# Grouped-query attention: another share of the exponentials for VectorE, and V in other units

## The chip, the cores and the metric

The kernel runs on one core of one Trainium2 chip. The time is the device time of one execution in microseconds; the median of several runs counts. The core's engines work side by side, each through its own queue in order: TensorE (PE) for matrix products, ScalarE (ACT), VectorE (DVE), GpSimd (POOL), and SyncE (SP), which here only starts transfers.

## The reference

Attention with shared keys and values: batch 8, 512 positions, 32 query heads, 8 key/value heads (four query heads share one), dimension 64, all in fp32.

```python
scores = np.einsum('bhqd,bhkd->bhqk', Q, K_expanded) * scale      # scale = 1/8
weights = np.exp(scores - np.max(scores, axis=-1, keepdims=True))
weights = weights / (np.sum(weights, axis=-1, keepdims=True) + 1e-10)
output = np.einsum('bhqk,bhkd->bhqd', weights, V_expanded)
```

## The kernel before, in words

The fast path (`fast_path`) leaves the maximum out, computes exp(scores) as it is, and checks at the end that all sums lay between 64 and 57344; if not, `general_path` computes everything again. The order of the work is written out by hand: each engine takes its instructions in the order of the program text.

**Jobs.** The work is 64 jobs, j = 0 to 63, eight for each batch entry, one for each key/value head. A job has two pairs of query heads, i = 0 and 1. For each pair, each of four key chunks kc and each head m of the pair there is one block of scores, 128 keys x 512 queries: 16 blocks in all. They come from TensorE into PSUM, and their exponentials go into the tile `pt` as fp16, keys on the partitions. Then TensorE multiplies `pt` with V (`pv`, L365): V has a 65th column of ones, so that each output carries the sum of its weights. Of a pair's 64 such matmuls, those that use the last-made blocks of `pt` come last (`blocks`, L358).

**Who makes the exponentials.** ScalarE makes most of them, two blocks at a time (`act_tile`, L296; L302), from the PSUM tiles `s_ps` (two buffers). The first two or three blocks of pair 1 are made otherwise (`WIDE`, L41: three in a wide job, which is 4 <= j < 62 with j % 5 != 2, 47 jobs; two in the others, here called narrow jobs). The steps of this second way are:

- `exp_d` (L306, L313): VectorE turns scores in the PSUM tile `d_ps` (one buffer) into the bits u of a rough fp16 exponential.
- `exp_d2` (L320): VectorE takes the fraction f (L325); GpSimd makes a factor g (L330) and the product w of g and f (L336). Where `odd` is true (L324: a wide job in front of a narrow one, and job 62), VectorE makes g, and only w is left to GpSimd.
- `exp_d4` (L346, L349): VectorE adds w to u, which gives the block of `pt`.

**The order in one job.** `exp_d4` of a job is done in the middle of the next job, and so are all its PV matmuls. In job j (L570 to L630, last = j - 1): ScalarE tile 0; two blocks for VectorE and their conversion; tile 1; a check; PV of pair 0 of the last job with tile 2's scores between its halves; `norm` (L402: the reciprocal of the sums at L417, and the product that empties the one PV buffer into `o_sb` at L422); tile 3; in a wide job the single half tile 4, in one bank of `d_ps`; the transposes of a later job's Q into the other bank (`trans_q`, L207); `exp_d4` of the last job; `exp_d2` of this job; the copy of the transposed Q (L220); g, where it is VectorE's; PV of pair 1 in pieces between tiles 5 and 6; where the next job is wide, the scores and the conversion of its third block (L622); `norm` of pair 1.

**Loads and checks.** Q, K and V come by DMAs that GpSimd issues and that convert to bf16, in jobs listed by hand (`LOADS`, L275). V goes straight into its padded tile `vt` (65 columns a head). K is transposed by DMAs of SP's queue (`dma_k`, L190, in the jobs of `KEYS`, L269). `check_v` (L236, L238) takes the largest magnitude of one chunk of V, 32 times. `check_sums` (L395, L388) compares 16 pairs' sums with the limits, every five jobs.

Of the kernel before, what the change touches and what calls it, by code (L numbers as in the profile page):

```python
# [33 lines left out]
SUM_LO = 64.0  # L34
SUM_HI = 57344.0
V_HI = 1.0e15
NLAST = 16
LAST_SUMS = NLAST * 2 * 4


WIDE = lambda j: 4 <= j < 62 and j % 5 != 2  # L41

# [25 lines left out]
def fast_path(ctx, tc, Q, K, V, out, flag, ident):  # L68
# [13 lines left out]
    const_pool = ctx.enter_context(tc.tile_pool(name="const", bufs=1))  # L82
    qnat_pool = ctx.enter_context(tc.tile_pool(name="qnat", bufs=4))
    knat_pool = ctx.enter_context(tc.tile_pool(name="knat", bufs=2))
    qt_pool = ctx.enter_context(tc.tile_pool(name="qt", bufs=3))
# [10 lines left out]

    ok = const_pool.tile([128, SPB * 2 * SC], FP32, name="ok")
    okv = const_pool.tile([128, B * SC], FP32, name="okv")
    okall = const_pool.tile([128, 1], FP32, name="okall")
# [4 lines left out]
    vt = [const_pool.tile([128, SC, KV, D + 1], BF16, name=f"v{j}") for j in range(2)]  # L104
# [4 lines left out]
    kn, qn, kt, qt, twice = {}, {}, {}, {}, {}  # L109

# [8 lines left out]

    def load_v(b, lo=0):  # L120
        to = vt[b % 2][:, :, lo:, 0:D]
        of = V[b, :, lo:, :].rearrange("(p sc) g d -> p sc g d", p=128)
        if lo:
            for sc in range(SC):
                nc.gpsimd.dma_start(out=to[:, sc], in_=of[:, sc])
        else:
            nc.gpsimd.dma_start(  # L127
                out=to.rearrange("p sc g d -> p (sc g) d"),
                in_=of.rearrange("p sc g d -> p (sc g) d"),
            )  # L130

# [103 lines left out]

    def check_v(b, sc):  # L236
        n = b * SC + sc
        nc.vector.tensor_reduce(  # L238
            out=okv[:, n:n + 1], in_=vt[b % 2][:, sc, :, 0:D], op=ALU.max, axis=AX.XY,
            apply_absolute_value=True,  # L240
        )

    NJOB = NU * 2
    DPAIR = NPAIR - 1

    def taken(j):
        return 3 if WIDE(j) else 2

# [3 lines left out]
    def act_tiles(j):  # L252
# [7 lines left out]

    CHECKS = {
        (j, at): divmod(n, SC) for n, (j, at) in enumerate(
            [(j, 0) for j in (3, 4, 6, 7, 8, 11, 12, 16, 17, 21, 22, 23, 26, 27, 31, 32)]
            + [(j, 0) for j in (36, 37, 38, 41, 42, 46, 47, 48, 51, 52, 56, 57, 60, 61, 62)]
            + [(62, 1)]
        )
    }

    KEYS = dict(zip((4, 10, 16, 26, 36, 41, 50), range(1, B)))  # L269

# [24 lines left out]

    def act_tile(j, n, spare=None):  # L296
        group = act_tiles(j)[n]
        i, kc, lo = group[0]
        ps = s_pool.tile([128, 2, S], FP32, name="s_ps") if spare is None else spare
        for _, _, m in group:  # L300
            scores(j, ps[:, m, :], i, kc, m)
        return nc.scalar.activation(  # L302
            out=jobs[j]["pt"][:, i, kc, lo:, :], in_=ps[:, lo:, :], func=EXP, scale=scale
        )

    def exp_d(j, lo, hi, ps, other=None):  # L306
        st = jobs.setdefault(j, {})
        if "u" not in st:
            for name, dtype in (("u", I16), ("f", I16), ("g", BF16), ("w", BF16)):
                st[name] = dve_pool.tile([128, 3, S], dtype, name=name + "16")[:, 0:taken(j), :]  # L310
        for n in range(lo, hi):
            apart(scores(j, ps[:, n - lo, :], DPAIR, *divmod(d_block(j) + n, 2)), other)
        return lambda: nc.vector.tensor_scalar(  # L313
            out=st["u"][:, lo:hi, :], in0=ps[:, 0:hi - lo, :], scalar1=A_U, scalar2=B_U,
            op0=ALU.mult, op1=ALU.add,
        )

    def exp_d2(j, engine=None):  # L320
        st = jobs[j]
        by_bits = engine is None
        engine = engine or nc.gpsimd
        odd = j == NJOB - 2 or WIDE(j) and not WIDE(j + 1)  # L324
        nc.vector.tensor_single_scalar(  # L325
            out=st["f"], in_=st["u"], scalar=1023, op=ALU.bitwise_and
        )

        def factor():
            (nc.vector if odd else engine).tensor_scalar(  # L330
                out=st["g"], in0=st["f"], scalar1=-EXP_F1,
                scalar2=EXP_K * 2.0 ** (24 * by_bits), op0=ALU.add, op1=ALU.mult,
            )

        def product():
            engine.tensor_tensor(  # L336
                out=st["w"], in0=st["g"], in1=st["f"].bitcast(FP16) if by_bits else st["f"],
                op=ALU.mult,
            )
# [25 lines left out]
    def pv(j, i, lo, hi):  # L365
# [9 lines left out]
        for n in range(lo, hi):  # L375
# [3 lines left out]
                st["pt"][:, i, kc, m, qc * 128:(qc + 1) * 128],  # L379
                vt[b % 2][:, kc, 2 * gp + g, :],  # L380
# [4 lines left out]
    def in_bounds(outs, inv, first):  # L385
        ops = ((1.0 / SUM_HI, ALU.is_ge), (1.0 / SUM_LO, ALU.is_le))
        for out_, in1, (bound, op) in zip(outs, (first, outs[0]), ops):
            nc.vector.scalar_tensor_tensor(  # L388
                out=out_, in0=inv, scalar=bound, in1=in1, op0=op, op1=ALU.mult
            )  # L390


    full = []

    def check_sums():  # L395
        while full:
            flat = invs.pop(full.pop()).rearrange("p s m qc -> p (s m qc)")
            in_bounds((ok, ok), flat, ok)

    inv_last = const_pool.tile([128, NLAST, 2, SC], FP32, name="inv_last")  # L400

    def norm(j, i):  # L402
# [31 lines left out]
        if left > NLAST and n == SPB - 1:  # L434
            full.append(k)

    def all_checks():
        assert not full and not invs
        vmax = const_pool.tile([128, 1], FP32, name="vmax")
        nc.vector.tensor_reduce(out=vmax, in_=okv, op=ALU.max, axis=AX.X)  # L440
        okmin = const_pool.tile([128, 1], FP32, name="okmin")
        nc.vector.tensor_reduce(out=okmin, in_=ok, op=ALU.min, axis=AX.X)
        nc.gpsimd.tensor_scalar(
            out=okall, in0=vmax, scalar1=V_HI, scalar2=okmin, op0=ALU.is_le, op1=ALU.mult
        )

    LIMITS = ((1.0 / SUM_HI, ALU.is_ge), (1.0 / SUM_LO, ALU.is_le))
    rights = [const_pool.tile([128, LAST_SUMS], BF16, name=f"right{n}") for n in range(2)]

    def last_rights(lo, hi, first=None):  # L450
        inv = inv_last.rearrange("p s m qc -> p (s m qc)")
        for engine, right, (bound, op) in zip((first or nc.gpsimd, nc.gpsimd), rights, LIMITS):
            engine.tensor_scalar(
                out=right[:, lo:hi], in0=inv[:, lo:hi],
                scalar1=bound, scalar2=okall, op0=op, op1=ALU.mult,
            )
# [39 lines left out]
    for j in range(2):  # L496
        nc.gpsimd.memset(vt[j][:, :, :, D:D + 1], 1.0)
    load_k(0, 2, 4)
    load_k(0, 4, KV)
    load_q(0, 8, 16)  # L500
    load_v_head(0, 1)
    load_v(0, 2)
    nc.gpsimd.memset(ones, 1.0)
    nc.gpsimd.memset(ok, 1.0)

# [51 lines left out]
    two_keys(1)  # L557
    exp_d(0, 0, 2, d_tile())()
    act_tile(0, 3)
# [10 lines left out]
    for j in range(1, NJOB - 1):  # L570
# [8 lines left out]
        if j == 1:  # L579
            dma_k(0, 2)  # L580
        if j in KEYS:
# [12 lines left out]
        pv(last, 0, 0, 16)  # L594
# [6 lines left out]
        bank = d_tile()  # L601
        beside = act_tile(j, 4, bank) if taken(j) > 2 else None

# [30 lines left out]
    act_tile(j, 0)  # L634
    exp_d(j, 0, 2, d_tile())()
    all_checks()
# [139 lines left out]
```

## Time and profile before

| what | value |
|---|---|
| median of 3 runs | 404.75 us (404.59 to 404.81) |
| the profiled execution | 404.57 us |
| its span, first to last instruction | 402.8 us |
| granted TensorE clock, mean | 0.999 |
| ACTIVATE of 128x1024 (L302) | x400, mean 1122 ns |
| ACTIVATE of 128x512 (L302) | x47, mean 724 ns |
| conversion of 128x512 (L313) | x47, mean 684 ns |
| g on GpSimd, 128x1536 (L330) | x35, mean 1470 ns |
| w on GpSimd, 128x1536 (L336) | x47, mean 3098 ns |
| g on VectorE, 128x1536 (L330) | x12, mean 551 ns |

A row of a timeline gives the start in microseconds from the span's start, the duration, the engine, the line, the operation, what it writes and reads, and how many instructions the row holds; in brackets, how long the engine stood idle before it and for whom. A row of groups gives the count, the busy time in all, the mean duration in ns, and the idle time before. A row of stretches gives the stretch and its length, then the busy time (and count) of PE, its weight loads, DVE, ACT and POOL, the granted clock, the share of the DMA engines and GB/s.

### The profile page before, as it was taken

How to read it: one execution, taken by the hardware profiler on the slowest of the kernel's cores; microseconds unless marked ns; L12 is line 12 of the kernel's file. 1: busy time of each engine (PE TensorE's matmuls, PEld its weight loads, DVE VectorE, ACT ScalarE, POOL GpSimd, SP SyncE). 2: the span in 40 equal slices, each digit the busy share in tenths (PEclk: the TensorE clock that was granted, in tenths of full speed). 3: DMA queues.
4: the chain of work that ended last, by engine and by line, in shares of the span. 5: the costliest groups of instructions: out<-in, count | busy, mean ns of one | idle time of the engine just before them, and what ended most of it. 6: DMA issues, size and time to landing. Idle time of an engine off the chain costs nothing.

```text
span 402.8 us, 12997 instructions
## 1 busy us (share of the span) xinstructions
PE 375.8 (93%) x5670; PEld 228.0 (57%) x5670; DVE 366.4 (91%) x635; ACT 393.9 (98%) x454; POOL 286.8 (71%) x169
## 2 busy tenths in 40 slices
PE   7999999999999999999999999999999999999985
PEld 3565555555555555555555555555555555556554
DVE  4788998999999999999999999999999999999996
ACT  5999999999999999999999999999999999999995
POOL 9848577597587687687687686677776767765752
PEclk9999999999999999999999999999999999999999
DMA  9979999899999259999259999679369959222206
GB/s 145 163 190 182 91 288 225 164 211 237 184 214 206 107 88 247 192 239 182 107 84 226 168 227 197 208 109 252 110 170 202 175 169 128 107 106 106 88 34 201
DMA packets 82893, 67.73 MB, mean 168 GB/s; under 512 B 52752, under 2 KB 57872, under 8 KB 82832
## 3 DMA queue, kind: packets, MB, share of 16 engines
q0 software_dynamic: 45072, 24.91, 48.3%
q1 hardware_dynamic: 36688, 41.49, 36.6%
q8 instruction: 45, 0.74, 0.7%
q10 hardware_dynamic: 1072, 0.46, 0.4%
q14 instruction: 16, 0.13, 0.1%
HBM read 50.33 MB, written 33.55 MB: 208 GB/s over the span
## 4 chain that ended last, share of the span: by engine, by line
ACT 29%; PE 25%; POOL 24%; DVE 20%; issue 2%; ACTq 0%; DVEq 0%
ACT pt L302 28%; POOL w L336 16%; PE pv L377 12%; PE s_ps L284 9%; POOL g L330 8%; DVE pt L349 8%; DVE o_sb L422 4%; DVE f L325 4%; DVE qt L220 2%; PE d_ps L215 2%; DVE g L330 1%; DVE inv L417 1%; PE d_ps L284 1%; PE s_ps L510 1%; PE d_ps L377 0%
## 5 line engine op out<-in xcount | busy, mean ns | idle before, releaser
L302 ACT ACTIVATE pt<-s_ps 128x1024 f16<-128x1024 f32 x400 | 379.0, 1122 | 0.3 <-PE s_ps L284 0.2
L336 POOL TENSOR_TENSOR w<-g,f 128x1536 bf16<-128x1536 bf16 (+1 forms) x63 | 179.6, 2851 | 37.6 <-DVE g L330 33.4
L377 PEld LDWEIGHTS <-pt 128*128 128x128 f16 x4096 | 142.1, 98 | 81.2 <-issue 41.6
L377 PE MATMUL pv<-v,pt 128*128 128x65 bf16 x4032 | 177.8, 195 | 3.7 <-DVE o_sb L422 2.2
L284 PE MATMUL s_ps<-qt,kt 64*128 64x512 bf16 x746 | 152.3, 384 | 12.0 <-ACT pt L302 10.0
L330 POOL TENSOR_SCALAR g<-f 128x1536 bf16<-128x1536 int16 (+1 forms) x50 | 67.1, 1341 | 69.1 <-DVE f L325 69.0
L313 DVE TENSOR_SCALAR u<-d_ps 128x1024 int16<-128x1024 f32 (+1 forms) x111 | 109.9, 990 | 0.3
L284 PEld LDWEIGHTS <-kt 64*128 64x128 bf16 x960 | 50.2, 93 | 55.3 <-issue 31.5
L422 DVE TENSOR_TENSOR o_sb<-pv,inv 128x512 f32<-128x512 f32 x112 | 77.5, 692 | 3.9
L284 PE MATMUL d_ps<-qt,kt 64*128 64x512 bf16 x214 | 58.4, 376 | 3.5 <-ACT pt L302 0.3
L349 DVE TENSOR_TENSOR pt<-u,w 128x1536 uint16<-128x1536 int16 (+1 forms) x64 | 56.4, 882 | 2.3 <-POOL w L336 0.2
L220 DVE COPY qt<-d_ps 128x1024 bf16<-128x1024 bf16 x62 | 42.3, 684 | 0.0
L215 PEld LDWEIGHTS <-q_nat 128*128 128x128 bf16 x508 | 28.5, 98 | 23.8 <-issue 23.8
L417 DVE RECIPROCAL inv<-pv 128x8 f32<-128x8 f32 x112 | 23.1, 207 | 17.4 <-PE pv L377 16.0
L215 PE MATMUL d_ps<-ident,q_nat 128*128 128x128 bf16 x496 | 38.3, 220 | 0.0
L302 ACT ACTIVATE pt<-d_ps 128x512 f16<-128x512 f32 x47 | 34.0, 724 | 0.0
L325 DVE TENSOR_SCALAR f<-u 128x1536 int16<-128x1536 int16 (+1 forms) x64 | 33.3, 521 | 0.0
L238 DVE TENSOR_REDUCE okv<-v 128x1 f32<-128x512 bf16 x32 | 21.6, 676 | 0.0
L142 POOL DMA_DIRECT2D q_nat<-in_Q_dram x19 | 15.2, 801 | 0.1
L284 PE MATMUL s_ps<-qt,kt_first 64*128 64x512 bf16 x56 | 11.1, 396 | 1.9 <-ACT pt L302 1.5
L127 POOL DMA_DIRECT2D v<-in_V_dram x7 | 12.3, 1753 | 0.0
L422 DVE TENSOR_TENSOR o_sb<-pv,inv_last 128x512 f32<-128x512 f32 x14 | 9.7, 692 | 0.5
(61 smaller groups left out, 62.7 us busy)
## 6 DMA issues: line engine op xcount, KB each, us to landing
out_dram<-o_sb SPq DMA_DIRECT2D x31, 1024.0 KB, 6.1
q_nat<-in_Q_dram POOLq DMA_DIRECT2D x14, 1024.0 KB, 12.4
k_nat<-in_K_dram POOLq DMA_DIRECT2D x7, 512.0 KB, 7.5
v<-in_V_dram POOLq DMA_DIRECT2D x7, 512.0 KB, 13.6
kt<-kt SPq DMA_DIRECT2D x14, 256.0 KB, 4.0
q_nat<-in_Q_dram POOLq DMA_DIRECT2D x3, 512.0 KB, 7.5
out_dram<-o_sb SPq DMA_DIRECT2D x3, 256.0 KB, 2.4
kt<-k_nat SPq DMA_TRANSPOSE x32, 5.9
```

Source lines behind the costliest of these rows:

```text
L215: nc.tensor.transpose(ps[:, i, sc, :], qn[u // 2][:, sc, h:h + 2, :], ident),
L220: return done, lambda: apart(nc.vector.tensor_copy(out=qt[u][:, g, lo:hi, :], in_=ps[:, lo:hi, :, :].rearrange("p i sc c -> p i (sc c)")), ...
L284: return nc.tensor.matmul(ps, keys[64 * m:64 * m + 64, g if u == 0 else g ^ m, kc * 128:(kc + 1) * 128], qt[u][64 * m:64 * m + 64, g, i, : ...
L302: return nc.scalar.activation(out=jobs[j]["pt"][:, i, kc, lo:, :], in_=ps[:, lo:, :], func=EXP, scale=scale)
L313: return lambda: nc.vector.tensor_scalar(out=st["u"][:, lo:hi, :], in0=ps[:, 0:hi - lo, :], scalar1=A_U, scalar2=B_U, op0=ALU.mult, op1=AL ...
L325: nc.vector.tensor_single_scalar(out=st["f"], in_=st["u"], scalar=1023, op=ALU.bitwise_and)
L330: (nc.vector if odd else engine).tensor_scalar(out=st["g"], in0=st["f"], scalar1=-EXP_F1, scalar2=EXP_K * 2.0 ** (24 * by_bits), op0=ALU.a ...
L336: engine.tensor_tensor(out=st["w"], in0=st["g"], in1=st["f"].bitcast(FP16) if by_bits else st["f"], op=ALU.mult,)
L349: nc.vector.tensor_tensor(out=st["pt"][:, DPAIR, :, :, :].rearrange("p kc m q -> p (kc m) q")[:, d_block(j):d_block(j) + n, :].bitcast(U16 ...
L377: nc.tensor.matmul(st["pv"][i][:, m, qc, :], st["pt"][:, i, kc, m, qc * 128:(qc + 1) * 128], vt[b % 2][:, kc, 2 * gp + g, :], start=(n < 2 ...
L417: nc.vector.reciprocal(out=inv, in_=sums[:, :, :, D:D + 1])
L422: nc.vector.tensor_tensor(out=osb[u][:, :, h:h + 2, :].rearrange("p qc m d -> p m qc d"), in0=sums[:, :, :, 0:D], in1=inv[:, :, :, None].t ...
```

## The change

1. **Another pattern of wide jobs.** `WIDE` is now 4 <= j < 62 with j % 8 < 7: 51 jobs. VectorE makes g in jobs `ALONE`: j >= 4 with j % 8 in 2, 4, 6.
2. **The third block is converted in its own job.** `odd_tile` takes the place of the half tile: it makes the scores of both heads into the two banks of one `d_ps` tile, ScalarE takes one of them, VectorE converts the other. The conversion in the job before is gone. In a wide job the transposes of Q stand behind tiles 5 and 6 now, and PV of pair 1 is cut at 12 of 32.
3. **V in units of 2^-16.** V and its column of ones are scaled by 2^-16. V is loaded into a contiguous tile `v_nat` (one buffer), and VectorE scales it into the padded tile (72 columns a head now) once for each batch entry; for the first entry GpSimd scales it in place, in three parts. `check_v` is gone.
4. **The check of the sums** takes a minimum, a maximum and a total of each full tile of reciprocals, once in eight jobs (j = 10, 18, ...); the limits are compared at the end.
5. **Loads at other jobs.** V and K of the next entry are issued in job 8b, two loads of Q in job 8b + 7, the transposes of K in job 8b + 3.

```diff
-WIDE = lambda j: 4 <= j < 62 and j % 5 != 2
+WIDE = lambda j: 4 <= j < 62 and j % 8 < 7
+ALONE = lambda j: j >= 4 and j % 8 in (2, 4, 6)
...
+    def load_v(b):
+        vn[b] = vnat_pool.tile([128, SC, KV, D], BF16, name="v_nat")
+        nc.gpsimd.dma_start(
+            out=vn[b], in_=V[b].rearrange("(p sc) g d -> p sc g d", p=128)
+        )
...
+    def units_v(b, lo=0, hi=KV):
+        to = vt[b % 2][:, :, lo:hi, 0:D]
+        if b:
+            nc.vector.tensor_single_scalar(out=to, in_=vn.pop(b), scalar=V_UNIT, op=ALU.mult)
         else:
+            nc.gpsimd.tensor_single_scalar(out=to, in_=to, scalar=V_UNIT, op=ALU.mult)
...
-    in_jobs(load_k, 1, [3, 8, 12, 23, 32, 38, 48])
-    in_jobs(load_q, 2, [3, 7, 8, 12, 17, 22, 23, 27, 32, 37, 38, 42, 47, 48])
-    in_jobs(load_v, 1, [4, 13, 18, 28, 33, 43, 53])
+    in_jobs(load_k, 1, [3])
+    in_jobs(load_q, 2, [3, 4])
+    in_jobs(load_q, 4, [j for b in range(B - 2) for j in 2 * [8 * b + 7]])
+    in_jobs(load_v, 1, [4])
...
+    def odd_tile(j, ps):
+        (i, kc, m), = act_tiles(j)[4]
+        scores(j, ps[:, 0, :], i, kc, 0)
+        scores(j, ps[:, m, :], i, kc, m)
+        st = jobs[j]
+        left = nc.scalar.activation(
+            out=st["pt"][:, i, kc, m:, :], in_=ps[:, m:, :], func=EXP, scale=scale
+        )
+        to_bits(st["u"][:, 2:3, :], ps[:, 0:1, :])
+        return left
...
-        odd = j == NJOB - 2 or WIDE(j) and not WIDE(j + 1)
+        odd = ALONE(j)
...
     def check_sums():
-        while full:
-            flat = invs.pop(full.pop()).rearrange("p s m qc -> p (s m qc)")
-            in_bounds((ok, ok), flat, ok)
+        k = full.pop()
+        flat = invs.pop(k).rearrange("p s m qc -> p (s m qc)")
+        for n, op in enumerate((ALU.min, ALU.max, ALU.add)):
+            nc.vector.tensor_reduce(out=found[:, n, k:k + 1], in_=flat, op=op, axis=AX.X)
...
-        cut = (11, 19) if taken(j) < 3 else (4, 18) if taken(last) < 3 else (4, 16)
+        cut = (12, 12) if taken(j) > 2 else (11, 19)
         act_tile(j, 0)
...
-        exp_d(j, 0, 2, d_tile())()
+        exp_d(j, d_tile())
         act_tile(j, 1)
-        if j % 5 == 3:
+        if j in SUMS:
             check_sums()
-        if (j, 0) in CHECKS:
-            check_v(*CHECKS[j, 0])
+        if j in UNITS:
+            units_v(UNITS[j])
+            if UNITS[j] + 1 < B:
+                load_v(UNITS[j] + 1)
+                load_k(UNITS[j] + 1)
         pv(last, 0, 0, 16)
         act_tile(j, 2)
         pv(last, 0, 16, 32)
...
         bank = d_tile()
-        beside = act_tile(j, 4, bank) if taken(j) > 2 else None
+        beside = None
+        if taken(j) > 2:
+            beside = odd_tile(j, bank)
+            act_tile(j, 5)
+            pv(last, 1, 0, cut[0])
+            act_tile(j, 6)
...
         exp_d4(last)
         rest = exp_d2(j)
-        copies = [read() for read in reads]
+        for read in reads:
+            read()
         if rest:
             rest()
-        if taken(j) == 2:
+        if not beside:
             act_tile(j, 4)
-        pv(last, 1, 0, cut[0])
-        act_tile(j, 5)
-        if beside:
+            pv(last, 1, 0, cut[0])
+            act_tile(j, 5)
             pv(last, 1, *cut)
-        if taken(j + 1) > 2:
-            exp_d(j + 1, 2, taken(j + 1), bank[:, 1:2, :], copies[0])()
-        if (j, 1) in CHECKS:
-            check_v(*CHECKS[j, 1])
-        if not beside:
-            pv(last, 1, *cut)
-        act_tile(j, 6)
+            act_tile(j, 6)
         pv(last, 1, cut[1], 32)
         norm(last, 1)
```

More of the change, by code (lines that the diff above doesn't have):

```diff
@@ L234, in piece @@
         pieces.append((bank, done, copy))
[L236 to L241, printed above, removed]
     NJOB = NU * 2
@@ L259, in fast_path @@
     jobs, osb, invs = {}, {}, {}
[L261 to L269, printed above, removed]
+    SUMS = [8 * b + 2 for b in range(1, B)]
+    UNITS = {8 * b: b for b in range(1, B)}
+    KEYS = {8 * b + 3 if b else 4: b + 1 for b in range(B - 1)}
     def in_jobs(load, first, jobs):
@@ L294, in open_job, with act_tile @@
         jobs.setdefault(j, {}).update(pt=pt, pv={})
-    def act_tile(j, n, spare=None):
+    def act_tile(j, n):
         group = act_tiles(j)[n]
         i, kc, lo = group[0]
-        ps = s_pool.tile([128, 2, S], FP32, name="s_ps") if spare is None else spare
+        ps = s_tile()
         for _, _, m in group:
@@ L304, in act_tile, with to_bits, exp_d @@
         )
[L306 to L315, printed above, removed]
-        )
+    def odd_tile(j, ps):
[5 more added lines that the diff above has]
+            out=st["pt"][:, i, kc, m:, :], in_=ps[:, m:, :], func=EXP, scale=scale
+        )
+        to_bits(st["u"][:, 2:3, :], ps[:, 0:1, :])
+        return left
+    def to_bits(out, in_):
+        nc.vector.tensor_scalar(
+            out=out, in0=in_, scalar1=A_U, scalar2=B_U, op0=ALU.mult, op1=ALU.add
+        )
+    def exp_d(j, ps):
+        st = jobs[j]
+        for name, dtype in (("u", I16), ("f", I16), ("g", BF16), ("w", BF16)):
+            st[name] = dve_pool.tile([128, 3, S], dtype, name=name + "16")[:, 0:taken(j), :]
+        for n in range(2):
+            scores(j, ps[:, n, :], DPAIR, *divmod(d_block(j) + n, 2))
+        to_bits(st["u"][:, 0:2, :], ps)
     def exp_d2(j, engine=None):
@@ L435, in norm @@
             full.append(k)
+    LEAST, MOST = 1.0 / SUM_HI / V_UNIT, 1.0 / SUM_LO / V_UNIT
     def all_checks():
         assert not full and not invs
[L439 to L447, printed above, removed]
+        for n, op in enumerate((ALU.min, ALU.max, ALU.add)):
+            nc.vector.tensor_reduce(out=seen_all[:, n:n + 1], in_=found[:, n, :], op=op, axis=AX.X)
+        right = 1.0
+        for n, (bound, op) in enumerate(((LEAST, ALU.is_ge), (MOST, ALU.is_le), (1.0e30, ALU.is_le))):
+            nc.gpsimd.tensor_scalar(
+                out=okall[:, n:n + 1], in0=seen_all[:, n:n + 1],
+                scalar1=bound, scalar2=right, op0=op, op1=ALU.mult,
+            )
+            right = okall[:, n:n + 1]
+    LIMITS = ((LEAST, ALU.is_ge), (MOST, ALU.is_le))
     rights = [const_pool.tile([128, LAST_SUMS], BF16, name=f"right{n}") for n in range(2)]
@@ L557, in fast_path @@
     two_keys(1)
-    exp_d(0, 0, 2, d_tile())()
+    exp_d(0, d_tile())
     act_tile(0, 3)
```

49 lines of the change are left out of this document (21 added, 28 removed).

## Prediction

> **What bounds the kernel now.** I read the page first, then the groups by form, then the timeline of jobs 30 to 34, which stand for the 58 jobs from 4 to 61. The page names ScalarE (ACT), busy in almost every microsecond and nearly never waiting; yet its chain of waits spreads over four engines:
>
> ```profile
> PE 375.8 (93%) x5670; PEld 228.0 (57%) x5670; DVE 366.4 (91%) x635; ACT 393.9 (98%) x454; POOL 286.8 (71%) x169
> ACT 29%; PE 25%; POOL 24%; DVE 20%; issue 2%; ACTq 0%; DVEq 0%
> ```
>
> ScalarE's instructions overlap, so being busy is not running at its own pace. The pace is in the timeline of ScalarE:
>
> ```profile
> 203.92 8.40 ACT L302 ACTIVATE pt<-s_ps 128x1024 f16<-128x1024 f32 x9
> 212.09 0.72 ACT L302 ACTIVATE pt<-d_ps 128x512 f16<-128x512 f32 x1
> 212.57 1.16 ACT L302 ACTIVATE pt<-s_ps 128x1024 f16<-128x1024 f32 x1
> ```
>
> Nine full exponentials take 212.09 - 203.92 = 8.17 us, 0.908 each (undelayed ones start 0.904 apart), and a half one 212.57 - 212.09 = 0.48. A wide job (three blocks off ScalarE) needs 6 x 0.904 + 0.48 = 5.90 us of it, a narrow one (two blocks) 7 x 0.904 = 6.33. Five jobs, four of them wide, would need 29.95. They take longer:
>
> ```profile
> 35.10:59.50 24.40, 23.09 (x355) 14.16 (x353) 23.03 (x40) 24.40 (x29) 17.48 (x10) 1.00 1.25 183
> 59.50:351.60 292.10, 277.33 (x4230) 168.01 (x4228) 273.62 (x467) 291.97 (x337) 214.68 (x109) 1.00 0.89 178
> 351.60:388.00 36.40, 34.20 (x521) 20.70 (x520) 34.70 (x60) 36.40 (x43) 23.07 (x10) 1.00 0.24 88
> ```
>
> These stretches run from one final addition of VectorE (DVE, L349, "d4" below) to another, over 4, 48 and 6 jobs. The middle one gives 292.1 / 48 = 6.085 us a job, 30.43 per five. So 0.48 us in five jobs is paid to something else. VectorE's order, in job 30's end and job 31, shows what:
>
> ```profile
> 193.29 0.96 DVE L349 TENSOR_TENSOR pt<-u,w 128x1536 uint16<-128x1536 int16 x1
> ...
> 195.24 0.68 DVE L313 TENSOR_SCALAR u<-d_ps 128x512 int16<-128x512 f32 x1
> 195.84 0.20 DVE L417 RECIPROCAL inv<-pv 128x8 f32<-128x8 f32 x1
> ```
> ```profile
> 199.50 0.96 DVE L349 TENSOR_TENSOR pt<-u,w 128x1536 uint16<-128x1536 int16 x1
> 200.37 0.55 DVE L325 TENSOR_SCALAR f<-u 128x1536 int16<-128x1536 int16 x1
> 200.84 0.69 DVE L220 COPY qt<-d_ps 128x1024 bf16<-128x1024 bf16 x1
> 201.44 0.55 DVE L330 TENSOR_SCALAR g<-f 128x1536 bf16<-128x1536 int16 x1
> 201.91 0.20 DVE L417 RECIPROCAL inv<-pv 128x8 f32<-128x8 f32 x1
> 202.14 0.69 DVE L422 TENSOR_TENSOR o_sb<-pv,inv 128x512 f32<-128x512 f32 x1
> 202.75 1.22 DVE L313 TENSOR_SCALAR u<-d_ps 128x1024 int16<-128x1024 f32 x1
> 203.88 0.68 DVE L238 TENSOR_REDUCE okv<-v 128x1 f32<-128x512 bf16 x1
> 204.52 0.21 DVE L417 RECIPROCAL inv<-pv 128x8 f32<-128x8 f32 x1
> 204.76 0.69 DVE L422 TENSOR_TENSOR o_sb<-pv,inv 128x512 f32<-128x512 f32 x1
> 205.37 0.95 DVE L349 TENSOR_TENSOR pt<-u,w 128x1536 uint16<-128x1536 int16 x1
> ```
> ```profile
> 194.81 1.47 POOL L330 TENSOR_SCALAR g<-f 128x1536 bf16<-128x1536 int16 x1 [1.55 <-DVE f L325]
> 196.37 3.10 POOL L336 TENSOR_TENSOR w<-g,f 128x1536 bf16<-128x1536 bf16 x1
> 202.07 3.10 POOL L336 TENSOR_TENSOR w<-g,f 128x1536 bf16<-128x1536 bf16 x1 [2.61 <-DVE g L330]
> ```
> ```profile
> 202.89 0.67 PE L377 MATMUL pv<-v,pt 128*128 128x65 bf16 x16 [0.21 <-DVE o_sb L422]
> 203.49 0.39 PE L284 MATMUL s_ps<-qt,kt 64*128 64x512 bf16 x2
> 203.81 0.67 PE L377 MATMUL pv<-v,pt 128*128 128x65 bf16 x16
> 204.41 0.39 PE L284 MATMUL s_ps<-qt,kt 64*128 64x512 bf16 x2
> 204.74 0.62 PE L215 MATMUL d_ps<-ident,q_nat 128*128 128x128 bf16 x8
> ```
>
> Two loops close from one d4 to the next. **The POOL loop:** d4, f, the factor g and the product w on GpSimd (POOL), d4: 199.50 - 193.29 = 6.21 us, with w ending at 199.47, right ahead of d4. **The PV loop**, where VectorE makes g: d4, f, the Q copy, g, the reciprocal and product that empty the one PV buffer (to 202.83), then PE's 16 PV matmuls at 202.89, scores, 16 more, the next reciprocal and product, d4: 205.37 - 199.50 = 5.87. GpSimd had ended w at 202.07 + 3.10 = 205.17, so here it is the PV loop that decides. ScalarE hangs on it: the scores at 203.49, between the PV halves, feed the exponential that starts at 203.92, which is 1.03 after the first PV matmul (call that P). In the old kernel such a job is followed by a narrow one, so its loop holds no conversion of a third block; slack comes back there.
>
> **The change part by part.** Times of one VectorE step are from start to start, since each starts some 0.08 before the end of the one ahead.
>
> *Four more wide jobs* (51 for 47): ScalarE needs 4 x (0.904 - 0.48) = 1.7 us less. That is a gain only where ScalarE sets the pace.
>
> *The third block is converted in its own job.* The 512-wide conversion (195.84 - 195.24 = 0.60) leaves its place behind the Q copy of the job before and stands between the first product of o_sb and d4. The scores it reads are issued behind the fourth ScalarE tile's, at P + 1.52 (204.41) and later, so it can't fill VectorE's idle time ahead of the reciprocal; it adds its 0.60 to every loop that runs into a wide job. In an ordinary wide loop it stood already, and the POOL loop's 6.21 hides it. The transposes of Q move behind ScalarE's last tile; tile 6's scores wait for tile 3's exponential to free its buffer, which in a late loop is at P + 1.03 + 0.90 + 1.12 (its mean duration) = P + 3.05; 0.33 later (204.41 to 204.74) come the transposes, 0.62 long, so they end at P + 4.0. The copy is due at d4 + 1.34 = P + 4.4. The room of 0.4 makes me cost them at nothing; without it, each wide loop would lose up to their 0.55 (204.74 to 205.29).
>
> *The factor on VectorE in j % 8 = 2, 4 and 6.* Each such job costs GpSimd 1.47 less and VectorE 201.91 - 201.44 = 0.47 more. GpSimd's loop would fall below 5.87. But jobs 3 and 5 behind them are wide now, so the PV loop holds both the factor and the conversion: 5.87 + 0.60 = 6.47, above ScalarE's 5.90. Only job 6 is followed by a narrow one.
>
> *The V path.* 32 checks leave VectorE:
>
> ```profile
> L238 DVE TENSOR_REDUCE okv<-v 128x1 f32<-128x512 bf16 x32 | 21.6, 676 | 0.0
> ```
>
> They stood where VectorE waits for PV (203.88 to 204.52, the reciprocal being due 0.71 after 203.81 whatever stands there), so their 21.6 us free nothing. The seven scalings take that place. No row shows one, so the bounds: at f's rate 2048/1536 x 0.47 = 0.63 us, which the check's 0.64 covers; at the check's rate 4 x 0.64 = 2.6, which is 1.9 too long, seven times. I take the low end, since f is the same kind of instruction on elements as wide. The Trainium skill, page "VectorE: DVE Perf Modes", section "The perf-mode tier table", gives 693 ns for a scalar operation over 2048 bf16 in SBUF; by that figure the sum would be the same, and no run here shows it yet. The three short reductions for the sums come in job 2, whose d4 waits for GpSimd anyway. GpSimd's in-place scalings in jobs 1 and 2 (256 and 1536 elements, under 1.5 us by its g) stand in its waits:
>
> ```profile
> 16.86 1.04 POOL L330 TENSOR_SCALAR g<-f 128x1024 bf16<-128x1024 int16 x1 [1.11 <-DVE f L325]
> ...
> 23.29 1.05 POOL L330 TENSOR_SCALAR g<-f 128x1024 bf16<-128x1024 int16 x1 [3.18 <-DVE f L325]
> ```
>
> The moved loads are issued one to four jobs early into GpSimd's waits; V's issue waits for the scaling (one buffer), with only K's issue and a g due 2 us later behind it. SP's queue keeps its order, with each K transpose four or five jobs ahead of its use. I cost these at nothing; without that cover it would be one issue (1.75 us by L127's old V row) in seven jobs.
>
> ```profile
> L127 POOL DMA_DIRECT2D v<-in_V_dram x7 | 12.3, 1753 | 0.0
> ```
>
> **The sum over eight jobs**, counted from P of job 0 (j % 8 = 0) to P of the next:
>
> ```profile
> 209.03 0.35 PE L377 MATMUL pv<-v,pt 128*128 128x65 bf16 x6
> ...
> 211.50 0.68 DVE L349 TENSOR_TENSOR pt<-u,w 128x1024 uint16<-128x1024 int16 x1
> ...
> 216.66 0.21 DVE L417 RECIPROCAL inv<-pv 128x8 f32<-128x8 f32 x1 [0.57 <-PE pv L377]
> ...
> 217.51 0.95 DVE L349 TENSOR_TENSOR pt<-u,w 128x1536 uint16<-128x1536 int16 x1
> ```
>
> - d4 in job 0 comes at P + 2.48 (205.37 - 202.89) plus the conversion 0.60: 3.08.
> - Behind a narrow job the next d4 comes 217.51 - 211.50 = 6.01 later: 9.09.
> - Five loops, jobs 1 to 5: 6.21, 6.47, 6.21, 6.47, 6.21 = 31.57: 40.66.
> - Job 6, factor on VectorE: from d4 to P 202.89 - 199.50 = 3.39: 44.05.
> - Narrow job 7, ScalarE's: 209.03 - 202.89 = 6.14: 50.19 us.
>
> The old kernel needs 8 x 6.085 = 48.68, so 1.51 more; six such groups (jobs 8 to 55) give +9.1. Jobs 4 to 7: 3.08 to the first d4, then to P 3.39 less 0.27 (its d4 is the short one), 3.08, 6.21, 3.39 and 6.14, sum 25.02, against 24.40 in the first stretch: +0.6. Jobs 56 to 61 end in a d4 at P + 40.66; now at 2.48 + 36.40 = 38.88 (the last stretch): +1.8. Start and tail I leave as they are. The sum is +11.5 (9.1 + 0.6 + 1.8): 404.57 (span 402.8 and 1.8 around it) becomes 416.0, to a tenth or so. The median of the runs, 404.75, lies 0.18 above the profiled execution, and I add nothing for that.
>
> **The rivals.**
>
> *ScalarE sets the pace* (the side on which it gets faster): freed of the checks, VectorE keeps every d4 loop under ScalarE's 5.90 us, the point from which it decides. Eight jobs then take 7 x 5.90 + 6.33 = 47.63, so -6.3 over six groups and about -1.4 at the ends: 397; if the old stalls stay and only the half tiles go, 404.6 - 1.7 = 402.9. For it: VectorE idles in jobs without a check (0.57 at 216.66), and loses more work than it gets. Against it: 5.87 was measured without a conversion inside. Chance 0.12.
>
> *The conversion finds room, the factor not*: the loops of 6.47 stay at 5.87. 15 such loops (two in each of six groups, three at the ends) give 15 x 0.60 = 9.0 back: 406.8. For it: the conversion's scores are ready early. Against: VectorE runs in order, and nothing stands idle between o_sb and d4 in the rows at 204.76. Chance 0.08.
>
> *The scaling runs at the check's rate*: 7 x 1.9 less about 0.2 of slack each, +12 more: 427. Chance 0.04.
>
> *It doesn't do what it says*: the new limits send it into the general path, a loop that no row shows, far above all these. Chance 0.01.
>
> **How the numbers follow.** Forecast 416.0 with chance 0.75, which holds a few tenths per loop either way: 410 to 420. Low end 405 takes in the second rival; the first and the two slow ones are left out, 0.17. A measurement of this kernel can tell about 0.2% (0.8 us) from no change: faster 0.12, within it 0.03 (the second rival's lower edge), slower 0.85 (0.75 + 0.05 + 0.04 + 0.01).
>
> **What the new profile would show.** d4 to d4 should be 6.4 to 6.5 us behind j % 8 = 2 and 4, 6.2 behind 1, 3 and 5, with ScalarE's starts over 1.3 apart at its third tile of jobs 3, 5 and 7, and PE waiting there for o_sb. V's scaling should last under 0.75. I am wrong if ScalarE's full tiles stay 0.90 to 0.92 apart throughout, or if the loop behind job 2 is 5.9.

## The result: 59 us slower, and the profile after

The changed kernel takes 463.72 us (463.70 to 463.89), the kernel before on the same chip 404.73: a ratio of 1.1459 (95% interval 1.1439 to 1.1479). The forecast was 416.0, its range 405 to 420. The sign was right, the size far off: +59.0 us instead of +11.5. The granted clock was 1.0 in the profiled execution, so nothing of it is the clock's.

The page of the changed kernel, busy times and chain:

```profile
PE 368.7 (80%) x5670; PEld 225.7 (49%) x5670; DVE 367.6 (80%) x632; ACT 401.0 (87%) x454; POOL 276.6 (60%) x163
...
ACT 50%; DVE 32%; PE 11%; issue 6%; POOL 1%; ACTq 0%; DVEq 0%; POOLq 0%
```

Over 462.0 us every engine has a smaller share than before, none of them 90%: the time has gone into waits. The groups of VectorE, with shapes kept apart, show where:

```profile
L318 DVE TENSOR_SCALAR u<-d_ps 128x512 int16<-128x512 f32 x51 | 35.3, 692 | 49.3 <-ACT pt L311 49.3
...
L139 DVE TENSOR_SCALAR v<-v_nat 128x2048 bf16<-128x2048 bf16 x7 | 7.8, 1121 | 0.0
```

The third block's conversion (L318) lasts 692 ns (684 before), but VectorE stands idle 49.3 us ahead of its 51 instances, and all of it is ended by L311, ScalarE's half exponential. V's scaling (L139) lasts 1121 ns in the mean where the forecast had 630. The waits of the changed kernel (engine and line, released by, total us, times, longest):

```profile
DVE u L318 <- ACT pt L311: 49.3, 51, 1.3
...
PE d_ps L226 <- DVE u L318: 39.5, 51, 0.8
ACT pt L301 <- ACT pt L301: 39.1, 47, 0.9
```

These three rows are one ring. The third names ScalarE itself as the one waited for; what ends that wait is the scores from TensorE, as the rows show. One wide loop of it, from ScalarE's tile 0 to the next tile 0, first ScalarE:

```profile
202.55 3.80 ACT L301 ACTIVATE pt<-s_ps 128x1024 f16<-128x1024 f32 x4 [0.89 <-ACT pt L301]
206.24 0.59 ACT L311 ACTIVATE pt<-d_ps 128x512 f16<-128x512 f32 x1
206.72 1.95 ACT L301 ACTIVATE pt<-s_ps 128x1024 f16<-128x1024 f32 x2
209.56 1.02 ACT L301 ACTIVATE pt<-s_ps 128x1024 f16<-128x1024 f32 x1 [0.88 <-ACT pt L301]
```

VectorE in the same loop:

```profile
205.24 0.69 DVE L425 TENSOR_TENSOR o_sb<-pv,inv 128x512 f32<-128x512 f32 x1
206.87 0.69 DVE L318 TENSOR_SCALAR u<-d_ps 128x512 int16<-128x512 f32 x1 [0.94 <-ACT pt L311]
207.48 0.95 DVE L359 TENSOR_TENSOR pt<-u,w 128x1536 uint16<-128x1536 int16 x1
```

And TensorE (the first row is the first PV matmul, P in the prediction):

```profile
203.38 0.66 PE L387 MATMUL pv<-v,pt 128*128 128x65 bf16 x16 [0.23 <-DVE o_sb L425]
...
205.12 0.38 PE L283 MATMUL d_ps<-qt,kt 64*128 64x512 bf16 x2
...
207.61 0.61 PE L226 MATMUL d_ps<-ident,q_nat 128*128 128x128 bf16 x8 [0.76 <-DVE u L318]
208.06 1.08 PE L387 MATMUL pv<-v,pt 128*128 128x65 bf16 x20
209.07 0.39 PE L283 MATMUL s_ps<-qt,kt 64*128 64x512 bf16 x2
```

The conversion's scores are issued at 205.12, and VectorE is free at 205.85. The conversion starts at 206.87, right behind the half exponential's end (206.83), though the two read different banks of the tile. The Q transposes go into the bank that the conversion reads, so they start at 207.61; PV's tail (20 of the pair's 32 matmuls; 64 is the number of a whole job) and the next tile 0's scores stand behind them on TensorE. The scores end at 209.46, tile 0 starts at 209.56, and ScalarE stands idle 0.88 before it. Round the ring: four tiles 3.69 (202.55 to 206.24), half exponential to conversion 0.63, to the transposes 0.74, to PV's tail 0.45, to the scores 1.01, to tile 0 0.49: 7.01 us, the same as the loop of VectorE's final additions below.

All loops behind job 8, as distances between the starts of the final additions (`exp_d4`), in us. A column is the job j % 8 in which the loop ends; 7 is the narrow job. The measured row is the same to 0.01 in all six groups of eight jobs, job 8 to job 55:

| | 1 | 2 | 3 | 4 | 5 | 6 | 7 | 0 | eight jobs |
|---|---|---|---|---|---|---|---|---|---|
| forecast | 6.01 | 6.21 | 6.47 | 6.21 | 6.47 | 6.21 | 12.61 with 0 | | 50.19 |
| changed kernel | 6.75 | 7.01 | 7.48 | 7.01 | 7.48 | 7.01 | 5.85 | 8.05 | 56.63 |

The 7.48 are loops in which VectorE makes g as well. The chain then runs from the final addition over g to the product into `o_sb`, for which PV waits 0.70 us, and on to the half exponential by the scores of tile 2, for which ScalarE waits. TensorE and ScalarE in such a loop:

```profile
210.86 0.66 PE L387 MATMUL pv<-v,pt 128*128 128x65 bf16 x16 [0.70 <-DVE o_sb L425]
```

```profile
211.89 1.94 ACT L301 ACTIVATE pt<-s_ps 128x1024 f16<-128x1024 f32 x2 [0.39 <-PE s_ps L283]
```

### The profile page after: what moved, and what is told of

It reads as the page before. It is cut to its first block, busy times and chain, and to the rows that moved or that the text cites. A ratio compares the mean times of both kernels' runs of the same rounds, so it can differ in the third digit from the quotient of the medians.

```text
span 462.0 us, 12947 instructions
## 1 busy us (share of the span) xinstructions
PE 368.7 (80%) x5670; PEld 225.7 (49%) x5670; DVE 367.6 (80%) x632; ACT 401.0 (87%) x454; POOL 276.6 (60%) x163
## 4 chain that ended last, share of the span: by engine, by line
ACT 50%; DVE 32%; PE 11%; issue 6%; POOL 1%; ACTq 0%; DVEq 0%; POOLq 0%
ACT pt L301 44%; DVE pt L359 9%; DVE u L318 8%; ACT pt L311 6%; PE pv L387 5%; DVE o_sb L425 4%; DVE f L335 4%; PE s_ps L283 3%; DVE qt L231 3%; DVE g L340 2%; PE d_ps L226 1%; PE s_ps L517 1%; POOL w L346 1%; DVE inv L420 1%; POOL g L340 0%
## 5 line engine op out<-in xcount | busy, mean ns | idle before, releaser
L346 POOL TENSOR_TENSOR w<-g,f 128x1536 bf16<-128x1536 bf16 (+1 forms) x63 | 183.4, 2911 | 80.6 <-DVE g L340 77.2
L318 DVE TENSOR_SCALAR u<-d_ps 128x1024 int16<-128x1024 f32 (+1 forms) x115 | 113.0, 983 | 49.3 <-ACT pt L311 49.3
L283 PE MATMUL s_ps<-qt,kt 64*128 64x512 bf16 x738 | 144.2, 383 | 5.8 <-ACT pt L301 5.2
L340 POOL TENSOR_SCALAR g<-f 128x1536 bf16<-128x1536 int16 (+1 forms) x40 | 54.2, 1354 | 91.5 <-DVE f L335 91.3
L283 PEld LDWEIGHTS <-kt 64*128 64x128 bf16 x960 | 45.2, 93 | 62.6 <-issue 41.4
L226 PEld LDWEIGHTS <-q_nat 128*128 128x128 bf16 x508 | 32.4, 97 | 52.9 <-issue 52.9
L283 PE MATMUL d_ps<-qt,kt 64*128 64x512 bf16 x222 | 42.9, 377 | 4.7
L311 ACT ACTIVATE pt<-d_ps 128x512 f16<-128x512 f32 x51 | 31.1, 610 | 0.0
L340 DVE TENSOR_SCALAR g<-f 128x1536 bf16<-128x1536 int16 (+1 forms) x24 | 13.0, 541 | 0.1
L139 DVE TENSOR_SCALAR v<-v_nat 128x2048 bf16<-128x2048 bf16 x7 | 7.8, 1121 | 0.0
```

The source lines that it names most:

```text
L226: nc.tensor.transpose(ps[:, i, sc, :], qn[u // 2][:, sc, h:h + 2, :], ident),
L283: return nc.tensor.matmul(ps, keys[64 * m:64 * m + 64, g if u == 0 else g ^ m, kc * 128:(kc + 1) * 128], qt[u][64 * m:64 * m + 64, g, i, : ...
L311: left = nc.scalar.activation(out=st["pt"][:, i, kc, m:, :], in_=ps[:, m:, :], func=EXP, scale=scale)
L318: nc.vector.tensor_scalar(out=out, in0=in_, scalar1=A_U, scalar2=B_U, op0=ALU.mult, op1=ALU.add)
L340: (nc.vector if odd else engine).tensor_scalar(out=st["g"], in0=st["f"], scalar1=-EXP_F1, scalar2=EXP_K * 2.0 ** (24 * by_bits), op0=ALU.a ...
L346: engine.tensor_tensor(out=st["w"], in0=st["g"], in1=st["f"].bitcast(FP16) if by_bits else st["f"], op=ALU.mult,)
```

## The experiments

The theory after the result: some 41 to 48 of the 59 us are the conversion's wait for ScalarE's read of the same tile, and what is left is about the forecast's sum. The rivals: that the forecast's chain itself was mis-sized (the factor and the conversion in one loop, or the place of the conversion), or that V's path costs most of it.

**1. Without the wait.** The program's `apart` declares two instructions independent because they are in different banks of one tile. Here it is said of the two readers too; nothing else changes.

```diff
-        to_bits(st["u"][:, 2:3, :], ps[:, 0:1, :])
+        apart(to_bits(st["u"][:, 2:3, :], ps[:, 0:1, :]), left)
...
-        nc.vector.tensor_scalar(
+        return nc.vector.tensor_scalar(
```

> The changed kernel, with the third block's conversion declared independent of ScalarE's half exponential (they read different banks of one tile), so that it waits for its own scores only. Theory A (the 59 us are this wait, about 1.0 us in each wide job, and beneath it lies the chain of the recorded forecast, with the scaling at 1.1 us and the slower start on top): 416 to 423 us, full ScalarE tiles in most jobs without the 0.9 us gap behind the half one. Rival B (the new order of PE's and VectorE's work is what is late, and the wait only shows where VectorE would wait anyway): over 445 us.

Measured 417.24 us (417.03 to 417.30), a ratio of 1.0315 (1.0298 to 1.0333). The wait was 46.5 us of the 59. Three final additions of this kernel, on VectorE:

```profile
174.58 0.96 DVE L359 TENSOR_TENSOR pt<-u,w 128x1536 uint16<-128x1536 int16 x1
...
180.43 0.68 DVE L318 TENSOR_SCALAR u<-d_ps 128x512 int16<-128x512 f32 x1
181.03 0.95 DVE L359 TENSOR_TENSOR pt<-u,w 128x1536 uint16<-128x1536 int16 x1
...
187.29 0.96 DVE L359 TENSOR_TENSOR pt<-u,w 128x1536 uint16<-128x1536 int16 x1 [0.21 <-POOL w L346]
```

The conversion now stands right ahead of the addition, with no idle time. The loops are 6.45 (with VectorE's g) and 6.26 (with GpSimd's, which VectorE waits 0.21 for): the forecast had 6.47 and 6.21. Eight jobs take 5.92 + 6.20 + 6.45 + 6.26 + 6.45 + 6.26 + 5.86 + 6.90 = 50.30, against 50.19 forecast. The same 48 jobs in rows of stretches, first the changed kernel, then this one:

```profile
65.97:405.77 339.80, 271.86 (x4224) 166.66 (x4224) 275.09 (x469) 297.48 (x337) 197.76 (x98) 1.00 0.60 148
```

```profile
61.85:363.44 301.59, 268.58 (x4225) 166.38 (x4223) 273.11 (x469) 293.03 (x337) 197.62 (x99) 1.00 0.70 169
```

Every engine's work is the same to 1.5%; only the length differs, by 38.2 us. The transposes' wait is gone from the waits of this kernel as well, so the forecast's room of 0.4 for them holds once the conversion is on time.

**2. The wait in the old pattern.** The changed kernel with the old choice of wide jobs:

```diff
-WIDE = lambda j: 4 <= j < 62 and j % 8 < 7
+WIDE = lambda j: 4 <= j < 62 and j % 5 != 2
...
-        odd = ALONE(j)
+        odd = j == NJOB - 2 or WIDE(j) and not WIDE(j + 1)
```

> The changed kernel, its wait kept, with the old pattern of wide jobs (j % 5 != 2) and VectorE's factor only in front of a narrow job. Theory A (the wait costs about 1.0 us in each wide job whatever the pattern): loops from one final addition to the next of 6.75, 7.01, 7.01, 5.85 and about 7.75, in all 448 to 462 us. Rival C (the new pattern with its three factors on VectorE is what hurts): under 430 us.

Measured 463.31 us (460.88 to 464.61), a ratio of 1.1456 (1.1428 to 1.1485), 1.3 above the expected range. Five jobs have loops of 6.74, 7.01, 7.01, 5.85 and 8.05; the last was expected at about 7.75. The wait is there as before:

```profile
DVE u L318 <- ACT pt L311: 44.3, 43, 1.3
```

It costs about the same in a pattern that never puts the factor and the conversion into one loop. As long as the wait is there, the pattern makes next to no difference; what it costs without the wait is in experiment 4.

**3. The half block in a tile of its own.** Here the two readers don't share a tile at all, with no declaration: ScalarE's half goes into a buffer of `s_ps`.

```diff
+        own = s_tile()
         scores(j, ps[:, 0, :], i, kc, 0)
-        scores(j, ps[:, m, :], i, kc, m)
+        scores(j, own[:, m, :], i, kc, m)
         st = jobs[j]
         left = nc.scalar.activation(
-            out=st["pt"][:, i, kc, m:, :], in_=ps[:, m:, :], func=EXP, scale=scale
+            out=st["pt"][:, i, kc, m:, :], in_=own[:, m:, :], func=EXP, scale=scale
         )
```

> The changed kernel with no declaration, but ScalarE's half exponential reads its block from a tile of its own (one of the two s_ps buffers), so that VectorE's conversion shares no tile with it. Theory A (the two readers of one tile are put in order): VectorE's wait for ScalarE at the conversion is gone, and the time is 416 to 430 us, the upper part if the s_ps buffers, which now turn over once more in each wide job, hold ScalarE's next tile up by 0.2 us. Rival D (what e1 took away was something else that the declaration also dropped): over 445 us.

Measured 439.27 us (439.12 to 440.62), a ratio of 1.0870 (1.0850 to 1.0891). This is neither the theory's range (416 to 430) nor the rival's (over 445). The conversion's wait for ScalarE is gone, as the theory says, but the price of the buffer was put too low. The waits of this kernel:

```profile
PE s_ps L283 <- ACT pt L301: 40.5, 102, 0.8
...
DVE qt L231 <- PE d_ps L226: 25.1, 51, 0.9
```

With one more tile in each wide job going through the two buffers, TensorE waits 40.5 us for a free one, the transposes stand behind that in its queue, and VectorE waits 25.1 us for them. The wait that the buffer removed comes back, in part, in another place.

**4. The factor in one job of eight.** Experiment 1 with VectorE's g only in the job ahead of the narrow one:

```diff
-ALONE = lambda j: j >= 4 and j % 8 in (2, 4, 6)
+ALONE = lambda j: j >= 4 and j % 8 == 6
```

> As e1_no_read_wait, and VectorE makes the factor only in j % 8 = 6 (and job 62). Theory A's chain: the loops of 6.47 become the POOL loop's 6.21, so 2 to 5 us less than e1. Rival (GpSimd is the one that lacks time, and the factor on VectorE is worth its place): 2 us or more above e1.

Measured 413.06 us (412.50 to 413.31), a ratio of 1.0214 (1.0197 to 1.0231): 4.2 less than experiment 1. The loops of 6.45 become 6.20, GpSimd's. So VectorE's factor costs time in jobs 2 and 4 of eight: beside a conversion it exchanges a loop of 6.20 set by GpSimd for one of 6.45 set by VectorE.

**5. The V path alone.** The kernel before, with V in units, its scaling, the missing checks of V and the new check of the sums; jobs, conversion and loads as they were.

```diff
-        if (j, 0) in CHECKS:
-            check_v(*CHECKS[j, 0])
+        if j in UNITS:
+            units_v(UNITS[j])
...
+    UNITS = {8 * b: b for b in range(1, B)}
```

> The kernel before with only the V path and the check of the sums changed (V scaled, no checks of V); the pattern of wide jobs, the factor and the conversion are the old ones. Theory A (the checks stood in VectorE's wait for PV; the scaling of 1.1 us is 0.5 too long for that place, seven times, and GpSimd's scaling in place delays the start): 405 to 410 us. Rival (VectorE's 21.6 us of checks were worth time): under 403 us.

Measured 410.69 us (410.57 to 410.74), a ratio of 1.0153 (1.0136 to 1.0170): a step that the forecast priced at nothing costs 6.3 us. That is 0.7 above the expected range, which took 1.1 us for a scaling; here they last up to 2.21. VectorE, then GpSimd, in one job that scales:

```profile
107.34 2.21 DVE L136 TENSOR_SCALAR v<-v_nat 128x2048 bf16<-128x2048 bf16 x1
109.47 0.20 DVE L407 RECIPROCAL inv<-pv 128x8 f32<-128x8 f32 x1
```

```profile
105.90 3.10 POOL L331 TENSOR_TENSOR w<-g,f 128x1536 bf16<-128x1536 bf16 x1
```

GpSimd's product ends at 109.00, and the scaling 0.55 later, at 109.55.

**6. The scaling where GpSimd is idle.** Experiment 5 with the scaling in narrow jobs, right behind the final addition, which itself waits for GpSimd's product:

```diff
-    UNITS = {8 * b: b for b in range(1, B)}
+    UNITS = dict(zip((7, 12, 22, 32, 37, 47, 52), range(1, B)))
...
-    in_jobs(load_v, 1, [4, 13, 18, 28, 33, 43, 53])
+    in_jobs(load_v, 1, [4, 8, 13, 23, 33, 38, 48])
...
-        if j in UNITS:
-            units_v(UNITS[j])
...
         exp_d4(last)
+        if j in UNITS:
+            units_v(UNITS[j])
```

> As e3_v_path_alone, with the seven scalings of V put right behind VectorE's final addition in narrow jobs, where GpSimd has just ended its product and waits. Theory P (a scaling makes no way while GpSimd runs a tensor instruction: it lasted 0.55 us plus its overlap with GpSimd's product in every run): 0.5 to 0.75 us each, in all 404.5 to 408 us. Rival (the padded output makes the scaling slow by itself): over 1.0 us each, 408 us or more.

Measured 406.46 us (406.43 to 407.96), a ratio of 1.0051 (1.0032 to 1.0070); the profiled execution took 407.96. VectorE:

```profile
330.39 0.95 DVE L344 TENSOR_TENSOR pt<-u,w 128x1536 uint16<-128x1536 int16 x1
331.26 0.69 DVE L136 TENSOR_SCALAR v<-v_nat 128x2048 bf16<-128x2048 bf16 x1
331.86 0.42 DVE L320 TENSOR_SCALAR f<-u 128x1024 int16<-128x1024 int16 x1
```

The same instruction lasts 0.69 (0.685 to 0.782 over the seven) instead of 2.21, and 4.2 of the 6.3 us come back.

**7. The new pattern with the conversion in its old place.** Experiment 5 with the new `WIDE` and `ALONE`; the conversion stays in the job before.

```diff
-WIDE = lambda j: 4 <= j < 62 and j % 5 != 2
+WIDE = lambda j: 4 <= j < 62 and j % 8 < 7
+ALONE = lambda j: j >= 4 and j % 8 in (2, 4, 6)
...
-        odd = j == NJOB - 2 or WIDE(j) and not WIDE(j + 1)
+        odd = ALONE(j)
```

> As e3_v_path_alone, with the new pattern (seven wide jobs of eight, the factor on VectorE in three), but the third block still converted in the job before. Theory A's chain (conversion and factor in one PV loop cost 6.47 wherever the conversion stands in it): 412 to 421 us, within 4 us of e1. Rival (it is the new place of the conversion and the transposes that costs): within 3 us of e3.

Measured 412.36 us (412.34 to 412.51), a ratio of 1.0195 (1.0178 to 1.0212), 4.9 below experiment 1 and 1.7 above experiment 5. The theory's range holds the time, but its "within 4 us of e1" doesn't, and the rival's "within 3 us of e3" does: the new place costs something too. By the totals the two can't be told apart, since V's scaling weighs on both sides. The loops tell more: 5.99, 6.19, 6.46, 6.26, 6.45, 6.26, 5.86 and 6.09, sum 49.56. The 6.45 of the factor and the conversion are there in either place; what differs is in the main the last loop, 6.90 in experiment 1. That loop on VectorE, first experiment 1, then this one:

```profile
205.87 0.95 DVE L359 TENSOR_TENSOR pt<-u,w 128x1536 uint16<-128x1536 int16 x1
...
210.25 1.16 DVE L139 TENSOR_SCALAR v<-v_nat 128x2048 bf16<-128x2048 bf16 x1
...
212.17 0.68 DVE L318 TENSOR_SCALAR u<-d_ps 128x512 int16<-128x512 f32 x1
212.76 0.68 DVE L359 TENSOR_TENSOR pt<-u,w 128x1024 uint16<-128x1024 int16 x1
```

```profile
203.09 0.95 DVE L346 TENSOR_TENSOR pt<-u,w 128x1536 uint16<-128x1536 int16 x1
...
204.90 0.68 DVE L310 TENSOR_SCALAR u<-d_ps 128x512 int16<-128x512 f32 x1
...
207.57 0.77 DVE L138 TENSOR_SCALAR v<-v_nat 128x2048 bf16<-128x2048 bf16 x1
...
209.18 0.68 DVE L346 TENSOR_TENSOR pt<-u,w 128x1024 uint16<-128x1024 int16 x1
```

In the old place the conversion for the first wide job falls into the narrow job, at 204.90. In the new place it stands right ahead of the addition that ends the loop. It costs time in that one loop of eight; part of the 0.8 is the scaling (1.16 against 0.77), which meets more of GpSimd's product. That product, first in experiment 1, then here:

```profile
208.74 2.12 POOL L346 TENSOR_TENSOR w<-g,f 128x1024 bf16<-128x1024 bf16 x1
```

```profile
205.67 2.12 POOL L333 TENSOR_TENSOR w<-g,f 128x1024 bf16<-128x1024 bf16 x1
```

**8. The new pattern, mended.** Experiment 7 with g on VectorE in one job of eight and the scaling behind the final addition of the narrow job:

```diff
-ALONE = lambda j: j >= 4 and j % 8 in (2, 4, 6)
+ALONE = lambda j: j >= 4 and j % 8 == 6
...
-    UNITS = {8 * b: b for b in range(1, B)}
+    UNITS = {8 * b - 1: b for b in range(1, B)}
...
-    in_jobs(load_v, 1, [4, 13, 18, 28, 33, 43, 53])
+    in_jobs(load_v, 1, [4] + [8 * b for b in range(1, B - 1)])
...
-        if j in UNITS:
-            units_v(UNITS[j])
...
         exp_d4(last)
+        if j in UNITS:
+            units_v(UNITS[j])
```

> As e5_pattern_old_place (new pattern, conversion in the job before), with VectorE's factor only in j % 8 = 6 and V's scaling in narrow jobs right behind the final addition. The chain: 5.99, five loops of 6.20, 5.86 and 6.44, 49.3 us in eight jobs against 48.68, and 2 us at the start: 407 to 411 us. Rival (with each of the faults mended the new pattern's four half tiles fewer for ScalarE pay): under 404 us.

Measured 409.76 us (409.67 to 409.88), a ratio of 1.0131 (1.0114 to 1.0148). Loops: 5.93, five of 6.20 to 6.21, 5.85 and 6.44, sum 49.25, against 48.68 for eight jobs of the kernel before. The five loops in a row at GpSimd's 6.20 are what seven wide jobs of eight pay; the 6.44 is the loop that holds V's scaling (in experiment 6 such loops take 6.44 to 6.53, those of narrow jobs without a scaling 6.08 to 6.14).

**9 and 10. More narrow jobs.** If GpSimd's loops cost, fewer of them might pay. The kernel before with every fourth, then every third job narrow:

```diff
-WIDE = lambda j: 4 <= j < 62 and j % 5 != 2
+WIDE = lambda j: 4 <= j < 62 and j % 4 != 2
```

> The kernel before with one other line: narrow jobs are those with j % 4 == 2, so a wide job with VectorE's factor comes each fourth job, in front of a narrow one. The chain of loops: 6.01, 6.20, 5.86 and 6.12, 24.2 us in four jobs against 6.085 a job, 402 to 403.5 us. Rival (ScalarE's work decides: three more full tiles in place of half ones): 405 us or more.

```diff
-WIDE = lambda j: 4 <= j < 62 and j % 5 != 2
+WIDE = lambda j: 4 <= j < 62 and j % 3 != 2
```

> As f1, with narrow jobs at j % 3 == 2. The loops would be 6.01, 5.86 and 6.12, 17.99 us, but ScalarE alone needs 2 x 5.90 + 6.33 = 18.13 and some 0.1 of gaps: 6.04 to 6.09 a job, 402 to 405 us. Rival (the loops through VectorE and GpSimd decide alone): under 401 us.

Measured 410.94 us (410.65 to 411.68), a ratio of 1.0150 (1.0133 to 1.0167), and 411.86 us (411.48 to 411.99), 1.0172 (1.0155 to 1.0189). Both miss. The first lies in the range of its rival (ScalarE's work decides), but not by the rival's reason: undisturbed groups of four take 24.38, or 6.095 a job, about the 6.085 of the kernel before, where ScalarE would need 6.01 by the forecast's 5.90 and 6.33. With every third job narrow, undisturbed groups take 18.41, or 6.137 a job. The loop out of a narrow job, put at 6.12, takes 6.3 in the first and 6.4 in the second; why was not taken further. What else is lost is, by the traces, a new overlap, which no run took out. The check of the sums stays in jobs j % 5 = 3, and six of its seven instances in the first, five in the second, now lie beside a wide job's product. VectorE, then GpSimd, with every fourth job narrow:

```profile
214.12 2.13 DVE L388 SCALAR_TENSOR_TENSOR ok<-inv,ok 128x128 f32<-128x128 f32 x2
216.16 0.20 DVE L417 RECIPROCAL inv<-pv 128x8 f32<-128x8 f32 x1
```

```profile
212.68 3.09 POOL L336 TENSOR_TENSOR w<-g,f 128x1536 bf16<-128x1536 bf16 x1
```

The pair takes 2.13 here; in the kernel before, where it met the last quarter of a microsecond of a narrow job's product, it took 0.76:

```profile
209.86 0.76 DVE L388 SCALAR_TENSOR_TENSOR ok<-inv,ok 128x128 f32<-128x128 f32 x2
```

No version that was run beats the kernel before.

## Why the prediction was wrong, step by step

**The step that failed** is the third block's: "The scores it reads are issued behind the fourth ScalarE tile's, at P + 1.52 (204.41) and later, so it can't fill VectorE's idle time ahead of the reciprocal; it adds its 0.60 to every loop that runs into a wide job." It took the conversion to wait for its scores alone. It waits for ScalarE's half exponential too, the other reader of the same tile. P being 203.38 in the loop shown, VectorE was free for it at P + 2.47 and it started at P + 3.49; experiment 1 puts this at 46.5 us. The code quoted ahead of the prediction shows it: `odd_tile` has no `apart` between the two reads, while the program uses `apart` where the transposes share that tile. The step asked what is queued ahead of the conversion on its engine, and not what else touches its tile.

**The chain behind it was right.** Without the wait the eight jobs are 50.30 against 50.19, the loop behind VectorE's g is 6.45 against 6.47, and the total is 417.24 against 416.0. Some of that nearness is luck. The span of experiment 1 is 12.5 us above the kernel before: 9.5 in jobs 8 to 55 (forecast 9.1), 1.0 in jobs 4 to 7 (0.6), 1.2 in jobs 56 to 61 (1.8), 1.4 ahead of job 4 and -0.5 at the end (both forecast at nothing), so errors of both signs meet. And the loops into jobs 7 and 0, 12.76 against 12.61, hold a scaling 0.5 longer than forecast.

**The factor**: right. Beside the conversion it lengthens the loop; experiment 4 gives 4.2 us back by taking it out.

**The transposes of Q at nothing**: right by themselves (experiment 1), but they handed on the conversion's lateness to TensorE and ScalarE.

**The V path at nothing**: wrong, in two terms. "I take the low end, since f is the same kind of instruction" gave 0.63; it measures 0.69 with GpSimd idle, but 1.12 in the mean in the changed kernel and up to 2.21 in experiment 5, since GpSimd's product ran beside it. The forecast's upper bound of 2.6 was nearer there, for a reason it didn't have. And GpSimd's scaling in place, "under 1.5 us by its g", takes 4.08. The start of the changed kernel on GpSimd, then on VectorE:

```profile
20.84 4.08 POOL L141 TENSOR_SCALAR v<-v 128x1536 bf16<-128x1536 bf16 x1
```

```profile
21.93 2.65 DVE L359 TENSOR_TENSOR pt<-u,w 128x1024 uint16<-128x1024 int16 x1
```

The addition beside it takes 2.65 instead of 0.68. In experiment 1 the loop that begins with it is 7.61 against 6.50 in the kernel before, 1.1 us at the start that the forecast left "as they are".

**The rivals.** ScalarE's pace never came: without the wait eight jobs take 50.30, where its pace would give 47.63. The conversion found no room in loops with the factor (6.45, not 5.87). The scaling at the check's rate was the right doubt at the wrong size. Two of the rivals' times are slips in the sum: 9.0 less than 416.0 is 407.0, not 406.8, and 12 more is 428, not 427.

**Where the 59.0 went**: 46.5 the read wait (changed kernel to experiment 1), 4.2 the factor beside the conversion (experiments 1 to 4), 8.6 the rest (experiment 4 less the kernel before, 404.42). This sums to 59.3, since the kernel before took 404.42 beside these runs and 404.73 beside the changed kernel. Of the rest the V path takes 6.3 in the old pattern (experiment 5), and how it and the row of 6.20 loops share it in the new one was not taken apart.

## What to carry to other kernels

Where two engines read one tile, look for the order between the reads: in different banks these two needed none (experiment 1), but the program may be given one, and the later reader then inherits every delay of the earlier. Before pricing a moved instruction, list every instruction that touches its tile, not only the producer of its input and the queue of its engine. And price an SBUF-to-SBUF instruction on VectorE by a row with the same neighbour on GpSimd: V's scaling took up to four times as long beside GpSimd's product (2.80 us in experiment 2, 0.69 with GpSimd idle in experiment 6).

## What the runs showed of the hardware

**V's scaling makes no way beside GpSimd's product.** Where the product is still running when it starts, it ends 0.55 us behind the product: overlaps of 0.22, 0.61 and 1.66 us gave 0.77 (experiment 7), 1.16 (experiment 1) and 2.21 (experiment 5); with GpSimd idle it lasts 0.69 (experiment 6). GpSimd, which had started first each time, loses nothing: its product takes 3.09 to 3.10 over three blocks, and 2.12 over two, beside the scaling or not. The Trainium skill, page "SBUF — State Buffer", section "SBUF: two separate sides", says that GpSimd shares a pair of ports, as an exclusive lock, with VectorE's operations that run in a two-port mode or have two inputs in SBUF: who starts first keeps it for the whole instruction, the other is blocked. The scaling and the pair of checks agree. The Trainium skill, page "VectorE: DVE Perf Modes", section "The perf-mode tier table", gives 693 ns for such an operation; the trace of experiment 6, with GpSimd idle, has 685 to 782, and beside GpSimd it doesn't hold.

**Not all is blocked.** The product that writes `o_sb`, with one input in PSUM, lasts 692 ns in the mean over the 112 instances of the changed kernel, 0.69 us each, beside GpSimd's products and away from them. The conversions of 128x512 from PSUM last 0.68 us in experiment 1, again beside them and away.

**An exception in size**: the addition of 2.65 us ended at 24.58, and GpSimd's scaling at 24.92. By that rule it should have ended behind; the ends of GpSimd's instructions are rough in a trace, and this was not taken further.

**GpSimd's scaling in place over rows of a padded tile** takes 4.08 us for 1536 elements a partition (changed kernel, experiment 6), where its g, from one contiguous tile to another, takes 1.47.
